# A two-layer diffusion transformer with 32 experts: rows in plain column order, weights in pairs of rows, splits 2,048 wide

## The chip, the cores and the metric

One core of a Trainium2 chip. The metric is the time of one execution on the device, in microseconds (us). TensorE (PE) multiplies; its weight loads are listed apart as PEld. VectorE (DVE), ScalarE (ACT) and GpSimd (POOL) do elementwise work, and SyncE (SP) issues most DMAs. Each engine takes its instructions strictly in the order in which the program was laid down. An instruction that has to wait holds up all those behind it on its engine.

## What is computed

Two layers over 1,024 latent tokens of width 1,024 and 256 context tokens: grouped-query attention in layer 0, a Fourier mix in layer 1, each followed by a mixture of 32 experts, of which every token uses two.

```python
for i in range(DEPTH):
    ...
    h = _modulate(x, norm_mix[i], sh1, sc1)
    ...
    x = x + g1 * y
    x = x + g2 * _hier_moe(_modulate(x, norm_ffn[i], sh2, sc2), *moe_p)
...
def expert_block(args):
    xblk, e = args
    return (jax.nn.silu(xblk @ w1[e]) * (xblk @ w3[e])) @ w2[e]
```

`w1[e]` and `w3[e]` are 1024x512 in fp32 and `w2[e]` is 512x1024, so an expert reads 6 MB.

## The kernel before

**Precision.** A product of fp32 matrices is made from high and low parts. ACT casts a weight to `wh` (a rounded type), DVE subtracts to get `wl`, and PE adds three products for each block of 128 rows: rows' high part by `wh` (L206), high by `wl` (L207), low by `wh` (L208).

**Weights of an expert.** They come in six pieces of 1 MB, two of each matrix, issued on SP's queue at L190. A piece fills a tile of 128 partitions by 2,048 values, or a list of two tiles 1,024 wide where a buffer of another phase is borrowed. A piece is split in two quarters 1,024 wide, by `quarter`: one cast (L1224) and one subtraction (L1229) each. One quarter in twelve is subtracted on POOL rather than on DVE. Five buffers of `wh` and five of `wl` (`NSP`) go round, and a quarter is prepared three ahead of its use (`AHEAD`).

**The loop over experts** (`phase_moe`). I call the halves of `w1` a0 and a1, those of `w2` b0 and b1, those of `w3` c0 and c1; a half is two quarters, 12 matmuls of 104 by 512. In steady state PE runs a0 of expert e; the four transposes `gT` of expert e-1's hidden rows (L1333); a1; the eight transposes of the next input rows (`xin`, L1304); b0 and b1 of expert e-1 into `py`; c0 and c1 of e. Each set of transposes goes to a PSUM tile `pt`, of which there are two. ACT takes the high part from it (`gh` L1336, `xh` L1305) and DVE the low part (`gl` L1337, `xl` L1306). From h1 and h3, ACT makes `s` (L1322) and DVE the hidden rows `gg` (L1325). DVE scales the output to `y`, in two operations (L1346); POOL adds it to its tokens in memory (L1347) and gathers the rows of later experts (L1293). The slot lists of coming experts come from one-hot tiles `oneh` on DVE (L1177) and products `pi` on PE (L1180).

**Column order.** A weight tile's partition p holds eight (or four) neighbouring rows of its matrix, 8 KB in a run. So the rows that meet it are kept in a permuted column order. Routing writes them so (`by_weights`, L956), with the shift B copied to that order on POOL (L929), and `gg` is permuted as it is written.

**What sets the order.** A scheduler orders the instructions of each engine when the program is built, from the order in the source, the pools' buffer counts and its own costs. Within an engine the order is then fixed.

Of the kernel before, what the change touches and what calls it, by code (L numbers as in the profile page):

```python
# [20 lines left out]
P = 128  # L21
D = 1024
# [44 lines left out]
NLATE, POOL_LAST = 5, 380  # L67
# [114 lines left out]
def load_piece(g, src, k, eng=None, order="(k p) n -> p k n"):  # L182

    t = raw_tile(g)
    eng = eng or g.nc.sync
    src = src.rearrange(order, p=P)
    ts = t if isinstance(t, list) else [t]
    k //= len(ts)
    for i, v in enumerate(ts):
        g.piece = eng.dma_start(v.rearrange("p (k n) -> p k n", k=k), src[:, k * i:k * i + k]).ins  # L190
    return t
# [728 lines left out]
def route_setup(g, mo, one, wk):  # L920
    nc, a, l = g.nc, g.a, mo.l
    r = Ctx()
    r.A2 = one.tile([P, D], F32, name="A2")
    r.B2 = one.tile([P, D], F32, name="B2")
    nf, b2 = (wk.tile([P, D], F32, name="h") for _ in range(2))
    bcast_row(g, r.A2, g.mod[l][0:1, 4 * D:5 * D])
    bcast_row(g, b2, g.mod[l][0:1, 3 * D:4 * D])
# [5 lines left out]
    for q in range(2):  # L933
        for nm, n0, n1 in (("rg", 0, NG), ("re", NG, NG + NE)):
            nc.gpsimd.dma_start(r.W[:, 4 * q:4 * q + 4, n0:n1],
                                a["moe_w_" + nm][l, q * 512:q * 512 + 512].rearrange("(p j) n -> p j n", j=4))
# [230 lines left out]
def slot_index(g, m, wk, pp, n, posm, val, tag):  # L1167

    nc = g.nc
    b = NE // 4 - 1 if n > 3 else 1  # L1170
    pi = pp.tile([CAP, n, 5], F32, name="pi")
    for e in range(n):
        oh = wk.tile([P, NT, CAP], BF, name="oneh", bufs=3)
        pe = posm(e)
        for t0, t1 in ((0, NT),) if n > 1 else ((0, NT - 2), (NT - 2, NT)):
            sh = [P, t1 - t0, CAP]
            nc.vector.tensor_tensor(oh[:, t0:t1], g.jrow[:, None, :].to_broadcast(sh),  # L1177
                                    pe[:, t0:t1, None].to_broadcast(sh), OP.is_equal)
        for t in range(NT):
            nc.tensor.matmul(pi[:, e], oh[:, t], val(e, t), start=(t == 0), stop=(t == NT - 1))  # L1180
    row = wk.tile([CAP, n], F32, name="row" + tag, bufs=1)
    nc.vector.tensor_scalar(row, pi[:, :, 1], float(SEQ), None, OP.add)
    idx = wk.tile([CAP, n], I32, name="idx" + tag, bufs=b)
    g.idx = nc.vector.tensor_add(idx, row, pi[:, :, 0]).ins
    gate = wk.tile([CAP, n], F32, name="gate" + tag, bufs=b)
    nc.vector.reduce_sum(gate, pi[:, :, 2:5], axis=AX.X)
    return idx, gate


class Moe:  # L1190
# [22 lines left out]
    def feed(self, eng=None):  # L1213

        while self.nl < min((self.ns - len(self.late)) // 2 + self.nraw, self.limit):
# [3 lines left out]
    def quarter(self, t, i):  # L1219

        nc = self.g.nc
        t = t[i] if isinstance(t, list) else t[:, i * 1024:(i + 1) * 1024]
        h, l = (self.hp.tile([P, 1024], F32R, name=n) for n in ("wh", "wl"))
        nc.scalar.copy(h, t)  # L1224
        if self.ns < NLATE:
            self.late.append((l, t, h))
            return h, l
        pool = self.ns > 11 and self.ns % 12 == 9 and (self.ns < POOL_LAST or not self.l)
        i = (nc.gpsimd if pool else nc.vector).tensor_sub(l, t, h)  # L1229
        if pool:  # L1230
            self.sub = i.ins
        else:
            self.vsub = i.ins
        return h, l

    def finish_late(self):

        for l, t, h in self.late:
            self.vsub = self.g.nc.vector.tensor_sub(l, t, h).ins
# [27 lines left out]
    def split(self, n):  # L1267

        while self.ns <= min(n, 2 * len(self.order) - 1):
            i, j = divmod(self.ns, 2)  # L1270
            self.sp[self.ns] = self.quarter(self.raw[i], j)
            if j:
                del self.raw[i]
# [3 lines left out]
    def get(self, n):  # L1277
        self.split(n + AHEAD)
        return self.sp.pop(n)

    def load(self, which, e, i, eng=None):
# [6 lines left out]
        t = load_piece(self.g, src, n // P, eng, "(p k) n -> p k n")  # L1288
# [8 lines left out]
    def xin(self, xg):  # L1297
        g, nc = self.g, self.g.nc
        xh = self.wk.tile([P, KD, CAP], F32R, name="xh")
        xl = self.wk.tile([P, KD, CAP], F32R, name="xl")  # L1300
        for q in range(2):
            pt = self.ps.tile([P, 4, CAP], F32, name="pt", bufs=2)
            for j in range(4):
                nc.tensor.transpose(pt[:, j], xg[:, (4 * q + j) * P:(4 * q + j + 1) * P], g.ident[:CAP, :CAP])  # L1304
            nc.scalar.copy(xh[:, 4 * q:4 * q + 4], pt)  # L1305
            nc.vector.tensor_sub(xl[:, 4 * q:4 * q + 4], pt, xh[:, 4 * q:4 * q + 4])  # L1306
# [12 lines left out]
    def hidden(self, h1, h3):  # L1319
# [4 lines left out]

        nc.vector.tensor_mul(gg.rearrange("t (i j p) -> t i p j", i=2, j=2), s_.rearrange("t (i p j) -> t i p j", i=2, j=2),  # L1325
                             h3.rearrange("t (i p j) -> t i p j", i=2, j=2))
        return gg

    def gT(self, gg):
        nc = self.g.nc  # L1330
        pt = self.ps.tile([P, 4, CAP], F32, name="pt", bufs=2)
        for j in range(4):
            nc.tensor.transpose(pt[:, j], gg[:, j * P:(j + 1) * P], self.g.ident[:CAP, :CAP])  # L1333
# [6 lines left out]
    def store(self, py, idx, gate):  # L1340
# [58 lines left out]
def phase_moe(g, mo, after=None, fin=None):  # L1399
# [4 lines left out]
    with mo.st as st:  # L1404
# [30 lines left out]
        for e in range(NE + 1):  # L1435
# [9 lines left out]
            if late:  # L1445
                gT = mo.gT(prev)
                py = [mo.psum("py", 2) for n in range(2)]
                for i in range(4):
                    p = mo.get(k + i)
                    for n in range(2):  # L1450
                        mo.mm(py[n], gT, p, i, n, 1)
# [39 lines left out]
            if e and not late:  # L1491
                py = [mo.psum("py", 2) for n in range(2)]
                for i in range(4):
                    p = mo.get(k + i)
                    for n in range(2):
                        mo.mm(py[n], gT, p, i, n, 1)
# [30 lines left out]
    with ExitStack() as st:  # L1527
# [10 lines left out]
        with tc.For_i(0, nx, 1):  # L1538
# [28 lines left out]
            for which in range(2):  # L1567
                hs.append(mo.psum(f"h{which}"))
                for i in range(2):
                    t = mo.load(which, bass.ds(re, 1), i)  # L1570
# [3 lines left out]
            py = [mo.psum("py", 2) for n in range(2)]  # L1574
            for i in range(2):
                t = mo.load(2, bass.ds(re, 1), i)
                for j in range(2):
                    w = mo.quarter(t, j)
                    for n in range(2):
                        mo.mm(py[n], gT, w, 2 * i + j, n, 1)  # L1580
# [531 lines left out]
```

## Time and profile before

| | |
|---|---|
| median of 3 runs | 2368.72 us (2367.48 to 2373.99) |
| the profiled execution | 2366.65 us |
| its span, first to last instruction | 2364.7 us |
| mean granted clock of PE | 0.954 |
| busy: PE, DVE, ACT, POOL | 2149.3, 1949.1, 1338.1, 1045.2 us |

The span divides into attention (to about 745 us), layer 0's projection and routing (to about 925), layer 0's experts (to about 1,500), the Fourier mix with layer 1's routing (to about 1,730) and layer 1's experts (to about 2,320). The experts are half of the time. A row of a group or timeline names the line, engine, operation and tiles of an instruction, and after an arrow in brackets what the engine waited for.

### The profile page before, as it was taken

How to read it: one execution, taken by the hardware profiler on the slowest of the kernel's cores; microseconds unless marked ns; L12 is line 12 of the kernel's file. 1: busy time of each engine (PE TensorE's matmuls, PEld its weight loads, DVE VectorE, ACT ScalarE, POOL GpSimd, SP SyncE). 2: the span in 40 equal slices, each digit the busy share in tenths (PEclk: the TensorE clock that was granted, in tenths of full speed). 3: DMA queues.
4: the chain of work that ended last, by engine and by line, in shares of the span. 5: the costliest groups of instructions: out<-in, count | busy, mean ns of one | idle time of the engine just before them, and what ended most of it. 6: DMA issues, size and time to landing. Idle time of an engine off the chain costs nothing. (4 is left out here: it accounts for less than half of the span.)

```text
span 2364.7 us, 29621 instructions
## 1 busy us (share of the span) xinstructions
PE 2149.3 (91%) x10250; PEld 1424.5 (60%) x10250; DVE 1949.1 (82%) x2822; ACT 1338.1 (57%) x1741; POOL 1045.2 (44%) x560
## 2 busy tenths in 40 slices
PE   6899999999999777999999999669699999999993
PEld 3677444444445565677777766447476777776662
DVE  4878566666675788999999999676899999998995
ACT  4733344443444235677776776443476777766773
POOL 2322566676767632334334442443233434423432
PEclk8999999999999898999999999879799999999997
DMA  8544434534333777999999999645599999999995
GB/s 304 186 160 141 165 112 134 180 112 134 115 114 129 255 250 267 359 361 331 353 345 343 362 361 336 213 192 213 218 307 348 339 343 351 354 345 347 348 366 198
DMA packets 152631, 614.22 MB, mean 260 GB/s; under 512 B 26961, under 2 KB 43993, under 8 KB 106461
## 3 DMA queue, kind: packets, MB, share of 16 engines
q1 hardware_dynamic: 110188, 546.87, 63.4%
q0 software_dynamic: 24672, 54.40, 9.0%
q10 hardware_dynamic: 17616, 11.01, 1.5%
q8 instruction: 82, 1.34, 0.2%
q14 instruction: 73, 0.59, 0.1%
HBM read 559.57 MB, written 78.44 MB: 270 GB/s over the span
## 5 line engine op out<-in xcount | busy, mean ns | idle before, releaser
L207 PE MATMUL h<-wl,xh 128*104 128x512 f32 x1024 | 411.6, 402 | 20.2 <-DVE wl L1229 16.9
L206 PE MATMUL h<-wh,xh 128*104 128x512 f32 x1024 | 410.4, 401 | 3.3 <-ACT wh L1224 3.3
L208 PE MATMUL h<-wh,xl 128*104 128x512 f32 x1024 | 406.6, 397 | 0.0
L684 POOL TENSOR_TENSOR acc<-acc,pe 128x1024 f32<-128x1024 f32 x125 | 298.8, 2391 | 96.4 <-ACT pe L673 94.0
L562 DVE TENSOR_REDUCE m<-sm 128x1 f32<-128x512 f32 x360 | 206.3, 591 | 136.4 <-PE sm L561 134.7
L673 ACT ACTIVATE pe<-st 128x1024 f32<-128x1024 f32 x160 | 163.7, 1023 | 261.8 <-PE st L659 259.9
L1293 POOL DMA_INDIRECT xg<-H,idx x64 | 116.4, 1819 | 290.8 <-PE pt L1304 182.9
L207 PEld LDWEIGHTS h<-wl,xh 128*104 128x104 f32 x1024 | 173.8, 170 | 93.5 <-DVE wl L1229 28.6
L1224 ACT CAST wh<-raw 128x1024 fp32r<-128x1024 f32 x196 | 199.8, 1054 | 48.4 <-DMA raw<-in_moe_w_dram 21.2
L1229 DVE TENSOR_TENSOR wl<-raw,wh 128x1024 fp32r<-128x1024 f32 x175 | 211.1, 1245 | 12.2 <-ACT wh L1224 12.0
L1224 ACT CAST wh<-wh 128x1024 fp32r<-128x1024 f32 x180 | 185.2, 1053 | 57.2 <-DMA wh<-in_moe_w_dram 22.8
L1229 DVE TENSOR_TENSOR wl<-wh 128x1024 fp32r<-128x1024 f32 x157 | 206.3, 1336 | 11.7 <-ACT wh L1224 11.4
L206 PEld LDWEIGHTS h<-wh,xh 128*104 128x104 f32 x1024 | 173.7, 170 | 65.9 <-ACT wh L1224 4.9
L1229 DVE TENSOR_TENSOR wl<-wl,wh 128x1024 fp32r<-128x1024 f32 x163 | 206.6, 1296 | 5.7 <-ACT wh L1224 5.4
L208 PEld LDWEIGHTS h<-wh,xl 128*104 128x104 f32 x1024 | 173.4, 169 | 59.7
L1347 POOL DMA_INDIRECT Xs<-y,idx x64 | 178.0, 2781 | 70.3 <-DVE y L1346 29.3
L1224 ACT CAST wh<-wl 128x1024 fp32r<-128x1024 f32 x172 | 177.2, 1053 | 51.8 <-PE h L208 23.9
L207 PE MATMUL py<-wl,gh 128*104 128x512 f32 x512 | 204.8, 401 | 0.2 <-DVE wl L1229 0.2
L208 PE MATMUL py<-wh,gl 128*104 128x512 f32 x512 | 202.2, 397 | 0.2 <-DVE gl L1337 0.2
L206 PE MATMUL py<-wh,gh 128*104 128x512 f32 x512 | 197.5, 404 | 2.0 <-ACT gh L1336 1.8
L664 PE MATMUL po<-pe,V 128*64 128x512 f32 x640 | 174.7, 624 | 0.4 <-ACT pe L673 0.4
L1224 ACT CAST wh<-X 128x1024 fp32r<-128x1024 f32 x124 | 129.6, 1053 | 56.3 <-PE h L208 45.3
(574 smaller groups left out, 4512.6 us busy)
## 6 DMA issues: line engine op xcount, KB each, us to landing
raw<-in_moe_w_dram SPq DMA_DIRECT2D x98, 1024.0 KB
wh<-in_moe_w_dram SPq DMA_DIRECT2D x90, 1024.0 KB
wl<-in_moe_w_dram SPq DMA_DIRECT2D x86, 1024.0 KB
qs<-in_moe_w_dram SPq DMA_DIRECT2D x96, 512.0 KB
raw<-in_w_mod_dram SPq DMA_DIRECT2D x43, 1024.0 KB
X<-in_moe_w_dram SPq DMA_DIRECT2D x37, 1024.0 KB
X<-in_moe_w_dram SPq DMA_DIRECT2D x50, 512.0 KB
QS<-qst ACTq DMA_DIRECT2D x32, 256.0 KB
```

Of the source, the lines that this page charges most:

```text
L206: nc.tensor.matmul(out, lh, wh, start=start, stop=False)
L207: nc.tensor.matmul(out, lh, wl, start=False, stop=False)
L208: nc.tensor.matmul(out, ll, wh, start=False, stop=stop)
L562: nc.vector.reduce_max(m3[:, h, qt, b:b + 1], ps[:, :kn], axis=AX.X)
L664: nc.tensor.matmul(po[64 * h:64 * h + 64], g.V[:, kt, g4 * HD:(g4 + 1) * HD], pe[:, h], start=(kt == 0), stop=(kt == NTA - 1))
L673: nc.scalar.activation(pe, ps, AF.Exp, scale=SCALE)
L684: eng.tensor_add(acc, acc, pe)
L1224: nc.scalar.copy(h, t)
L1229: i = (nc.gpsimd if pool else nc.vector).tensor_sub(l, t, h)
L1293: self.last = self.g.nc.gpsimd.indirect_dma_start(out=xg, out_offset=None, in_=self.H if src is None else src, in_offset=bass.IndirectOffs ...
L1347: return y, lambda: nc.gpsimd.indirect_dma_start(out=self.X, out_offset=bass.IndirectOffsetOnAxis(ap=idx, axis=0), in_=y, in_offset=None, ...
```

## The change

Five parts.

1. **Column order.** Routing's rows keep plain column order: `by_weights` is gone, B is loaded where it is used, and the router's weights come in 2 DMAs rather than 4.
2. **Pairs of rows.** A partition holds pairs of neighbouring rows. For `w1` and `w3` a piece is two runs of 4 KB in each partition; `w2` keeps 8 KB. The pieces in two tiles stay two DMAs with 4 KB runs.
3. **Splits in halves.** One cast and one subtraction 2,048 wide split a half (two of 1,024 each where the piece is in two tiles). Three buffers 2,048 wide take the place of five 1,024 wide, and a half is prepared two ahead. Of POOL's halves (one in six), DVE subtracts the first 1,024 and POOL the second, after one cast of 2,048.
4. **Transposes.** One `pt` tile of two banks serves `gT` and `xin` in turn. The transposes read every second value of a row. `xh` and `xl` are one operation of 832 columns each, and `gg` is a plain product.
5. **Outputs.** `py` is one tile of two banks and `y` one operation 1,024 wide.

There are also two `oneh` buffers where there were three.

```diff
-AHEAD = 3
-NSP = 5
-NSP_EARLY = 3
+NSP = 3
+NSP_EARLY = 2
...
-NLATE, POOL_LAST = 5, 380
+NLATE, POOL_LAST = 3, 190
...
-    nc.gpsimd.tensor_copy(by_weights(r.B2), b2.rearrange("t (q p j) -> t q p j", q=2, j=4))
+    bcast_row(g, r.B2, g.mod[l][0:1, 3 * D:4 * D])
...
-    x, a2 = (v[:, ns].rearrange("t (p j) -> t p j", j=4) for v in (x1, r.A2))
-    g.nc.vector.tensor_mul(by_weights(r.u[t])[:, n], x, a2)
+    g.nc.vector.tensor_mul(r.u[t][:, ns], x1[:, ns], r.A2[:, ns])
...
-        oh = wk.tile([P, NT, CAP], BF, name="oneh", bufs=3)
...
+            oh = wk.tile([P, NT, CAP], BF, name="oneh")
...
-    def quarter(self, t, i):
+    def half(self, t, ns=None):
...
-        h, l = (self.hp.tile([P, 1024], F32R, name=n) for n in ("wh", "wl"))
-        nc.scalar.copy(h, t)
...
+        h, l = (self.hp.tile([P, 2048], F32R, name=n) for n in ("wh", "wl"))
+        pool = ns is not None and ns > 5 and ns % 6 == 4 and (ns < POOL_LAST or not self.l)
...
     def get(self, n):
-        self.split(n + AHEAD)
-        return self.sp.pop(n)
+
+        i, j = divmod(n, 2)
+        self.split(i + NSP - 1)
+        return self.quarter(self.sp.pop(i) if j else self.sp[i], j)
...
-        t = load_piece(self.g, src, n // P, eng, "(p k) n -> p k n")
+        t = load_piece(self.g, src, n // P // 2, eng, "(k p j) n -> p k (j n)")
...
+        pt = self.ps.tile([P, 2, 512], F32, name="pt")
         for q in range(2):
-            pt = self.ps.tile([P, 4, CAP], F32, name="pt", bufs=2)
...
-            nc.scalar.copy(xh[:, 4 * q:4 * q + 4], pt)
-            nc.vector.tensor_sub(xl[:, 4 * q:4 * q + 4], pt, xh[:, 4 * q:4 * q + 4])
...
+        nc.scalar.copy(hv, pt)
+        nc.vector.tensor_sub(lv, pt, hv)
...
+        nc.vector.tensor_mul(gg, s_, h3)
...
-        pt = self.ps.tile([P, 4, CAP], F32, name="pt", bufs=2)
+        pt = self.ps.tile([P, 2, 512], F32, name="pt")[:, 0, :4 * CAP].rearrange("p (j n) -> p j n", j=4)
...
-        for n in range(2):
-            ns = slice(n * 512, (n + 1) * 512)
-            nc.vector.scalar_tensor_tensor(y[:, ns], py[n], gate, self.G2[:CAP, ns], OP.mult, OP.mult)
+        nc.vector.scalar_tensor_tensor(y, py.rearrange("t n c -> t (n c)"), gate, self.G2[:CAP], OP.mult, OP.mult)
```

The scheduler lays the new program down in another order. Before, DVE does this in the experts of layer 1, from one product `gg` on (`wl` is a subtraction of a weight part; the second name in each row is what it is made from):

```order
L1325 TENSOR_TENSOR gg<-s,h_18357 104x2x128x2
L1229 TENSOR_TENSOR wl<-wl,wh 128x1024
L1229 TENSOR_TENSOR wl<-raw,wh 128x1024 x2
L1337 TENSOR_TENSOR gl<-pt,gh 128x416
L1229 TENSOR_TENSOR wl<-raw,wh 128x1024 x2
L1229 TENSOR_TENSOR wl<-qs,wh 128x1024
L1306 TENSOR_TENSOR xl<-pt,xh 128x416 x2
```

In the changed kernel the same stretch of DVE is:

```order
L1339 TENSOR_TENSOR gg<-s,h_17052 104x512
L1238 TENSOR_TENSOR wl<-wl,wh 128x2048
L1238 TENSOR_TENSOR wl<-raw,wh 128x2048
L1351 TENSOR_TENSOR gl<-pt,gh 128x416
L1173 TENSOR_TENSOR oneh<-jrow,posb 128x832
L1238 TENSOR_TENSOR wl<-raw,wh 128x2048
L1321 TENSOR_TENSOR xl<-pt,xh 128x832
```

Between `gg` and `gl` stood two or three subtractions 1,024 wide; now there are in most experts two 2,048 wide.

On PE, before, at the end of a1 (the last `h`), with the input transposes (`pt` from `xg`) and the first three products of `py`:

```order
L208 MATMUL h_18412<-wh,xl 104x512
L1304 MATMUL pt<-ident,xg 128x104 x8
L206 MATMUL py<-wh,gh 104x512
L207 MATMUL py<-wl,gh 104x512
L208 MATMUL py<-wh,gl 104x512
```

And PE at the same place in the changed kernel:

```order
L210 MATMUL h_17595<-wh,xl 104x512
L208 MATMUL py<-wh,gh 104x512
L209 MATMUL py<-wl,gh 104x512
L1317 MATMUL pt<-ident,xg 128x104 x8
L210 MATMUL py<-wh,gl 104x512
```

The input transposes moved behind the first two products of `py`; in about twenty experts two groups of `pi` stand there too, between those products and the transposes. On ACT the cast of b1 stands ahead of `gh`, as it did before for its first quarter.

## Rows read from the trace of the kernel before

**Rows 1.** windows view of line 1325: stretch, us, busy (count), clock, DMA, GB/s

```profile
924.40:1493.90 569.50, 32.57 (x30) 0.99 0.98 350
1731.50:2299.30 567.80, 32.57 (x30) 1.00 0.99 348
```

**Rows 2.** same stretches, busy of PE, PEld, DVE, ACT, POOL

```profile
924.40:1493.90 569.50, 553.84 (x2710) 401.73 (x2709) 551.09 (x572) 415.70 (x479) 220.61 (x87) 0.99 0.98 350
1731.50:2299.30 567.80, 550.29 (x2704) 399.00 (x2702) 543.83 (x578) 415.82 (x479) 211.27 (x87) 1.00 0.99 348
```

**Rows 3.** waits of PE, layer 0: line, releaser: us, times, longest

```profile
PE h L207 <- DVE wl L1229: 10.1, 15, 1.7
...
PE pt L1304 <- DVE gl L1337: 1.2, 1, 1.2
```

**Rows 4.** timeline of PE, one expert: start us, us, instruction [idle before]

```profile
2053.83 0.58 PE L1333 MATMUL pt<-ident,gg 104*128 104x104 f32 x4 [0.91 <-DVE gg L1325]
...
2054.48 0.39 PE L207 MATMUL h<-wl,xh 128*104 128x512 f32 x1
...
2056.79 0.40 PE L208 MATMUL h<-wh,xl 128*104 128x512 f32 x1
...
2057.02 0.88 PE L1304 MATMUL pt<-ident,xg 104*128 104x104 f32 x8
...
2057.68 0.46 PE L206 MATMUL py<-wh,gh 128*104 128x512 f32 x1
```

**Rows 5.** timeline of ACT, same expert

```profile
2057.22 0.60 ACT L1322 ACTIVATE s<-h 104x512 f32<-104x512 f32 x1 [0.34 <-PE h L208]
```

**Rows 6.** timeline of DVE, same expert

```profile
2052.73 1.04 DVE L1325 TENSOR_TENSOR gg<-s,h 104x512 f32<-104x512 f32 x1
...
2053.62 2.33 DVE L1229 TENSOR_TENSOR wl<-wl,wh 128x1024 fp32r<-128x1024 f32 x2
...
2055.88 0.57 DVE L1337 TENSOR_TENSOR gl<-pt,gh 128x416 fp32r<-128x416 f32 x1
...
2066.26 1.40 DVE L1346 SCALAR_TENSOR_TENSOR y<-py,gate,G 104x512 f32<-104x512 f32 x2
```

**Rows 7.** groups by form: ns min/median/max, first and last start us

```profile
L1229 DVE TENSOR_TENSOR wl<-wl,wh x161: 1198/1216/3420, 929.3 to 2296.9; 128x1024 fp32r<-128x1024 f32 x161
...
L201 DVE TENSOR_TENSOR wl<-raw,wh x8: 2228/2292/3857, 31.5 to 747.7; 128x2048 fp32r<-128x2048 f32 x8
...
L200 ACT CAST wh<-raw x8: 1894/1908/1917, 29.6 to 744.8; 128x2048 fp32r<-128x2048 f32 x8
...
L1177 DVE TENSOR_TENSOR oneh<-jrow,posb x66: 360/1015/1971, 891.4 to 2113.5; 128x832 bf16<-128x832 bf16 x62, 128x624 bf16<-128x624 bf16 x2, 128x208 bf16<-128x208 bf16 x2
```

**Rows 8.** groups by form, plain operations 512 and 1,024 wide

```profile
L880 DVE TENSOR_TENSOR X<-mm,G x16: 653/681/692, 754.2 to 875.5; 128x512 f32<-128x512 f32 x16
...
L1983 DVE SCALAR_TENSOR_TENSOR X<-X,ftrs,V x8: 1277/1280/1287, 2330.9 to 2345.8; 128x1024 f32<-128x1024 f32 x8
```

**Rows 9.** group by form, weight loads of the input transposes

```profile
L1304 PEld LDWEIGHTS pt<-ident,xg x512: 137/140/231, 899.3 to 2287.8; 104*128 104x128 f32 x171
```

**Rows 10.** timelines of POOL and of DVE, both splitting

```profile
1239.24 2.62 POOL L1229 TENSOR_TENSOR wl<-raw,wh 128x1024 fp32r<-128x1024 f32 x1 [6.86 <-ACT wh L1224]
...
1239.51 3.44 DVE L1229 TENSOR_TENSOR wl<-raw,wh 128x1024 fp32r<-128x1024 f32 x1
```

**Rows 11.** groups by form, routing: rows into weight order, and the copy of B

```profile
L956 DVE TENSOR_TENSOR h<-X,A x32: 1032/1098/2884, 757.2 to 1685.8; 128x512 f32<-128x512 f32 x32
...
L929 POOL COPY B<-h x2: 2032/3007/3982, 745.6 to 1613.8; 128x1024 f32<-128x1024 f32 x2
```

**Rows 12.** windows view, all engines, layer 0's projection and routing

```profile
745.00:868.00 123.00, 101.61 (x483) 79.30 (x482) 105.44 (x168) 36.70 (x61) 84.20 (x58) 0.92 0.66 227
```

**Rows 13.** page, DMA queues: packets, MB, share of engines

```profile
q1 hardware_dynamic: 110188, 546.87, 63.4%
...
q10 hardware_dynamic: 17616, 11.01, 1.5%
```

More of the change, by code (lines that the diff above doesn't have):

```diff
@@ L924, in route_setup @@
     r.B2 = one.tile([P, D], F32, name="B2")
-    nf, b2 = (wk.tile([P, D], F32, name="h") for _ in range(2))
+    nf = wk.tile([P, D], F32, name="h")
     bcast_row(g, r.A2, g.mod[l][0:1, 4 * D:5 * D])
-    bcast_row(g, b2, g.mod[l][0:1, 3 * D:4 * D])
     bcast_row(g, nf, a["norm_ffn"][l:l + 1])
-    nc.gpsimd.tensor_copy(by_weights(r.B2), b2.rearrange("t (q p j) -> t q p j", q=2, j=4))
+    bcast_row(g, r.B2, g.mod[l][0:1, 3 * D:4 * D])
     r.gain = lambda: nc.vector.scalar_tensor_tensor(r.A2, r.A2, 1.0, nf, OP.add, OP.mult)
@@ L932, in route_setup @@
     nc.gpsimd.memset(r.W, 0.0)
[L933 to L936, printed above, removed]
+    nc.gpsimd.dma_start(r.W[:, :, 0:NG], a["moe_w_rg"][l].rearrange("(k p) n -> p k n", p=P))
+    nc.gpsimd.dma_start(r.W[:, :, NG:NG + NE], a["moe_w_re"][l].rearrange("(k p) n -> p k n", p=P))
     r.bias = one.tile([P, NG + NE], F32, name="br")
@@ L1172, in slot_index @@
     for e in range(n):
-        oh = wk.tile([P, NT, CAP], BF, name="oneh", bufs=3)
+        if e == 2 and n == 3:
+            oh = wk.tile([P, DE], F32, name="gg", bufs=1).bitcast(BF)[:, :NT * CAP].rearrange("p (t c) -> p t c", t=NT)
+        else:
+            oh = wk.tile([P, NT, CAP], BF, name="oneh")
         pe = posm(e)
@@ L1213, in feed, with rest, quarter @@
     def feed(self, eng=None):
-        while self.nl < min((self.ns - len(self.late)) // 2 + self.nraw, self.limit):
+        while self.nl < min(self.ns - len(self.late) + self.nraw, self.limit):
             self.raw[self.nl] = self.load(*self.order[self.nl], eng)
             self.nl += 1
-    def quarter(self, t, i):
+    def half(self, t, ns=None):
         nc = self.g.nc
-        t = t[i] if isinstance(t, list) else t[:, i * 1024:(i + 1) * 1024]
-        h, l = (self.hp.tile([P, 1024], F32R, name=n) for n in ("wh", "wl"))
-        nc.scalar.copy(h, t)
[L1225 to L1231, printed above, removed]
-        else:
-            self.vsub = i.ins
-        return h, l
+        h, l = (self.hp.tile([P, 2048], F32R, name=n) for n in ("wh", "wl"))
+        pool = ns is not None and ns > 5 and ns % 6 == 4 and (ns < POOL_LAST or not self.l)
+        if isinstance(t, list):
+            todo = [(l[:, c:c + 1024], v, h[:, c:c + 1024], pool and c) for c, v in zip((0, 1024), t)]
+        elif pool:
+            nc.scalar.copy(h, t)
+            todo = [(v[0], v[1], v[2], c) for c in (0, 1024) for v in [[u[:, c:c + 1024] for u in (l, t, h)]]]
+        else:
+            todo = [(l, t, h, 0)]
+        if isinstance(t, list) or not pool:
+            for v in todo:
+                nc.scalar.copy(v[2], v[1])
+        if ns is not None and ns < NLATE:
+            self.late.append(todo)
+        else:
+            self.rest(todo)
+        return h, l
+    def rest(self, todo):
+        for l, t, h, pool in todo:
+            i = (self.g.nc.gpsimd if pool else self.g.nc.vector).tensor_sub(l, t, h).ins
+            if pool:
+                self.sub = i
+            else:
+                self.vsub = i
+    @staticmethod
+    def quarter(t, j):
+        return [v[:, 1024 * j:1024 * j + 1024] for v in t]
     def finish_late(self):
-        for l, t, h in self.late:
-            self.vsub = self.g.nc.vector.tensor_sub(l, t, h).ins
+        for todo in self.late:
+            self.rest(todo)
         self.late = []
@@ L1267, in split @@
     def split(self, n):
[L1269 to L1273, printed above, removed]
+        while self.ns <= min(n, len(self.order) - 1):
+            self.sp[self.ns] = self.half(self.raw.pop(self.ns), self.ns)
             self.ns += 1
@@ L1446, in phase_moe @@
                 gT = mo.gT(prev)
-                py = [mo.psum("py", 2) for n in range(2)]
+                py = mo.ps.tile([CAP, 2, 512], F32, name="py")
                 for i in range(4):
@@ L1491, in phase_moe @@
             if e and not late:
-                py = [mo.psum("py", 2) for n in range(2)]
+                py = mo.ps.tile([CAP, 2, 512], F32, name="py")
                 for i in range(4):
@@ L1569, in phase_moe @@
                 for i in range(2):
-                    t = mo.load(which, bass.ds(re, 1), i)
+                    t = mo.half(mo.load(which, bass.ds(re, 1), i))
                     for j in range(2):
@@ L1573, in phase_moe @@
             gT = mo.gT(mo.hidden(*hs))
-            py = [mo.psum("py", 2) for n in range(2)]
+            py = mo.ps.tile([CAP, 2, 512], F32, name="py")
             for i in range(2):
-                t = mo.load(2, bass.ds(re, 1), i)
+                t = mo.half(mo.load(2, bass.ds(re, 1), i))
                 for j in range(2):
```

27 lines of the change are left out of this document (15 added, 12 removed).

## The prediction

> **What bounds the kernel now.** I read the windows view first, because the change lies almost wholly in the two loops over experts, and counted experts by their `gg`. Thirty go by in 569.50 us in layer 0 and in 567.80 us in layer 1 [rows 1], so an expert takes 18.98 and 18.93 us, and there are about 62 such periods in steady state. In the same stretches PE is busy for 553.84 and 550.29 us [rows 2]: 18.46 and 18.34 us an expert, with 0.52 and 0.58 us idle. DVE is busy for 551.09 and 543.83 us, and the DMA engines for 0.98 and 0.99 of the time. So three resources are full, and PE is the one with nothing left to give: its products alone, 72 at the step of 0.231 us (ten steps from 2054.48 to 2056.79 [rows 4]), are 16.63 us. What little PE waits for is mostly `wl` from DVE (10.1 us in fifteen waits). For the product `gl` ahead of the input transposes it waited once, 1.2 us [rows 3].
>
> Next I read the timelines of one expert, to see how `gl` is hidden. PE begins the transposes of the hidden rows at 2053.83 and gets to the input transposes at 2057.02 [rows 4]. DVE makes two quarter subtractions in 2.33 us after `gg`, then `gl`, which ends at 2055.88 + 0.57 = 2056.45 [rows 6]. So `gl` is 0.57 us early. This is the slack that the change has to live in.
>
> **The waits inside the new order.** This is the term that decides. Between `gg` and `gl` DVE now subtracts b0 and b1 whole. Three buffers go round, a0, a1, b0, so the cast of b1 takes the buffer of a0, and that is free when PE ends a0, just as it begins the hidden transposes (call this 0). A product's result releases ACT 0.20 us after the next instruction of PE has begun: next at 2057.02 [rows 4], `s` at 2057.22 [rows 5]. A 2,048-wide cast takes 1.91 us and a 2,048-wide subtraction 2.29 us (medians, rows of the attention phase), against 1.216 us for a quarter [rows 7]. So b1 is cast by 0.20 + 1.91 = 2.11 and subtracted by 4.40, and `gl` ends at 4.40 + 0.57 - 0.08 (two operations of DVE overlap at their joint: 2053.62 + 2.33 against 2055.88 [rows 6]) = 4.9. PE needs it after the hidden transposes and a1, 2057.02 - 2053.83 = 3.19 [rows 4], and two products of `py`, 0.46: at 3.65. There is now one `pt` tile, so the input transposes wait for `gl`; and the third product of `py` reads `gl` itself, so a second tile would gain little. The stall is 4.9 - 3.65 = **1.3 us an expert**, on PE, the engine with no slack. Queued behind it on PE are `py` and c0 and c1. DVE has gone on, but its next `xl` waits too.
>
> In before the buffers went round in quarters: the cast of b1's first quarter waited for half of a0, not all of it, and `gl` came ahead of b1's second quarter.
>
> How much of the 1.3 us shows? If nothing else of PE's idle time remains, the period is 18.46 + 1.3 = 19.76 and 18.34 + 1.3 = 19.64, which is 0.78 and 0.71 above before. If the old idle time stays on top, it is 1.3. If the stall hides wholly behind something, 0. I take 0.75, because the old waits are mostly for `wl` [rows 3], and a PE that arrives later finds those done. 62 x 0.75 = **+46 us** (0 to +81).
>
> **The one-hot tiles.** In about twenty experts two groups of `pi` stand between the two products and the input transposes, and the second reads a `oneh` that DVE makes behind `gl`, 1.015 us [rows 7]. The first `pi` group fills part of the stall. I count 0.5 us in each, **+10 us** (0 to +20).
>
> **What gets shorter on DVE.** A half is one subtraction of 2.29 us rather than two in 2.33; `y` is one of 1.28 (the 1,024-wide row [rows 8]) rather than 1.40 [rows 6]; `gg` falls from 1.04 [rows 6] to the plain 0.68 [rows 8]. With six halves that is 0.2 + 0.1 + 0.4 = 0.7 us an expert, `xl` a little besides. It lies beside PE's work except for `gg`, which the hidden transposes wait for. That wait was 0.91 us in the expert shown [rows 4], but all that PE idles is 0.5 us an expert [rows 2], and mostly for `wl` [rows 3], so I cost the gain at nothing in the sum. It is the first rival's ground.
>
> **Routing.** 32 operations wrote rows in weight order, at 1.098 us; plain ones of that size take 0.681 [rows 11, 8]. That is 32 x 0.42 = 13 us of DVE, and the two copies of B (2.0 and 4.0 us on POOL) go. In layer 0's stretch DVE is busy for 105.44 of 123 us [rows 12]; I let half count: **-7 us** (0 to -18).
>
> **Loads.** At most 256 pieces (four in each of 64 experts; those in two tiles have 4 KB already) change from 128 packets of 8 KB to 256 of 4 KB. From the two queues' rows [rows 13], a packet of 4,963 bytes took 218 ns of one engine (63.4% of 16 x 2,364.7 us by 110,188) and one of 625 bytes 32 ns. A line through both leaves some 5.5 ns that a packet costs whatever its size; 256 x 128 x 5.5 / 16 ns = 11 us. PE's stall gives DMA time to catch up, so I take **+3 us** (0 to +11).
>
> **Strided transposes.** The twelve transposes of an expert now read every second value. No row shows PE do that. The nearest is the write in weight order on DVE, 1.6 times the plain one. At that ratio the eight input transposes (0.66 us [rows 4]) and the four others would cost about 0.6 us an expert, +37 us; at the other end nothing, since what is read strided is the loaded operand (0.137 us [rows 9]), and loads run under the product before. I take 0 and keep the other end for the range.
>
> The Trainium skill (SBUF — State Buffer, Specifications (TRN2)) says that SBUF lines are 16 bytes and that full bandwidth wants at least two accesses in each. Steps of 16 bytes have one, and the old write in weight order was slow as that says. Steps of 8 bytes have two, so by this rule the transposes cost nothing, the end that I took.
>
> **The sum.** Against the profiled execution, 2366.65 us: +46 + 10 - 7 + 3 = +52 gives 2418.7. That execution is 2.1 us under the median of its runs, so a median of 2,420.8, say **2420 us**, +2.2%.
>
> **Rival 1: DVE's relief wins.** If the early experts are paced by DVE (0.97 busy [rows 2]), its 0.7 us come back as period, and if scheduling slack hides `gl`, PE sinks toward its busy time: 0.52 x 62 = -32, and -7 from routing, about 2330 us. For it: DVE is as full as PE. Against it: an in-order engine is held by its place in the chain, and b1's cast cannot start before a0 is done. It decides if `gl` ends less than 3.65 us after the hidden transposes begin, as when DVE does `gl` ahead of b1, which a few of the rows of the new order do. Chance 0.2.
>
> **Rival 2: the stall is covered.** DMA is at 0.98 of its time; if its arrivals set the period, PE's new stall takes the place of waits for weights, and only routing and the loads show: 2366.65 - 7 + 3 + 2.1, about 2365 us. For it: the full DMA engines. Against it: PE's idle time was half a microsecond, and the stall is more than twice that. Chance 0.1.
>
> **Rival 3: POOL and DVE block one another.** Where both subtracted at once, POOL took 2.62 us and DVE 3.44 against 1.216 [rows 10, 7]: DVE lost 2.2 us. Before, `y` stood beside most of POOL's work. Now DVE's 1,024 and POOL's are released by one cast, and a 2,048-wide subtraction follows `y` and stands ahead of `gg`. If one more microsecond is lost there in half of the experts, that is +31: about 2450 us. Chance 0.15.
>
> The Trainium skill (SBUF — State Buffer, SBUF: two separate sides) has a rule for this: DVE with two SBUF inputs and GpSimd take a shared port pair as an exclusive lock, for the whole instruction, and the other blocks. The 3.44 us agree: 2.2 us of waiting and 1.2 of work. By that rule, a wider DVE operation makes POOL wait longer too.
>
> **How the numbers follow.** Forecast as summed 0.55, rivals 0.2, 0.1 and 0.15. The range runs from **2345**, which takes in the part of rival 1 where some of the stall shows, to **2455**, which holds rival 3 and half of the price of strided transposes. A measurement of this kernel tells 0.3% (7 us) from no change: faster 0.2, same 0.1, slower 0.7.
>
> **What would show it.** Right: in the new trace the input transposes (or `pi`) wait for `gl` (or `oneh`) about 1 to 1.5 us in most experts, `gl` ends 4.5 to 5 us after the hidden transposes begin, the period is 19.5 to 20, and DMA's share falls under 0.96. Wrong: `gl` ends before PE's second product of `py`, or the period stays under 19 with DVE below 0.95. The strided transposes are shown by eight in more than 0.66 us; the loads, by waits for DMA.

## The result: slower, by less than half of the forecast

The changed kernel takes 2392.45 us (median of four runs, 2388.91 to 2395.71) against 2368.44 us for the kernel before (2367.48 to 2373.99). The ratio is 1.0096, with a 95% interval of 1.0072 to 1.012: 17 to 28 us slower. The forecast was slower, by 52 us, and the range of 2345 to 2455 holds the time. The size is off by a factor of two, and the parts of the sum are further off than the sum.

The profiled execution took 2388.91 us, its span 2386.7 us. The windows view again, line of `gg` (1339 now), thirty experts of each layer; it answers to [rows 1]:

```profile
912.30:1499.60 587.30, 20.22 (x30) 0.99 0.98 340
1732.80:2316.50 583.70, 20.24 (x30) 1.00 0.99 342
```

An expert takes 587.30 / 30 = 19.58 us and 19.46 us, 0.59 and 0.53 more than before: 34 us in all. The first `gg` comes at 912.3 rather than 924.4, and about 5 us are lost after the last.

All engines in the same stretches (busy of PE, PEld, DVE, ACT, POOL), which answers to [rows 2]:

```profile
912.30:1499.60 587.30, 566.67 (x2713) 414.35 (x2712) 523.67 (x381) 397.22 (x288) 257.02 (x88) 0.99 0.98 340
1732.80:2316.50 583.70, 562.29 (x2700) 410.85 (x2698) 523.66 (x407) 399.28 (x315) 243.67 (x88) 1.00 0.99 342
```

DVE's work fell as it should, from 551 us to 524 us in layer 0. DVE had time left and the kernel was slower. What PE and its weight loads wait for in layer 0 (line, releaser: us, times, longest) answers to [rows 3]:

```profile
PE pt L1317 <- DVE gl L1351: 15.4, 22, 1.7
PE pt L1347 <- DVE gg L1339: 2.4, 2, 1.2
PE h L209 <- DVE wl L1238: 1.3, 1, 1.3
...
PEld pt L1317 <- DVE gl L1351: 21.7, 23, 2.2
PEld pt L1347 <- DVE gg L1339: 14.0, 27, 1.6
```

The wait for `gl` ahead of the input transposes is now first, and the waits of products for `wl` went from 10.1 us to 1.3. The timelines of one expert of layer 1, on DVE, ACT and PE, answer to [rows 4 to 6]:

```profile
2080.83 0.68 DVE L1339 TENSOR_TENSOR gg<-s,h 104x512 f32<-104x512 f32 x1
2081.43 2.29 DVE L1238 TENSOR_TENSOR wl<-wl,wh 128x2048 fp32r<-128x2048 f32 x1
2084.21 2.29 DVE L1238 TENSOR_TENSOR wl<-wh 128x2048 fp32r<-128x2048 f32 x1 [0.50 <-ACT wh L1229]
2086.42 0.58 DVE L1351 TENSOR_TENSOR gl<-pt,gh 128x416 fp32r<-128x416 f32 x1
...
2082.28 1.91 ACT L1229 CAST wh<-wh 128x2048 fp32r<-128x2048 f32 x1 [0.90 <-PE h L210]
2084.09 0.50 ACT L1350 CAST gh<-pt 128x416 fp32r<-128x416 f32 x1
...
2082.03 0.61 PE L1347 MATMUL pt<-ident,gg 104*128 104x104 f32 x4
...
2085.50 0.40 PE L209 MATMUL py<-wl,gh 128*104 128x512 f32 x1
2087.06 1.20 PE L1317 MATMUL pt<-ident,xg 104*128 104x104 f32 x8 [1.16 <-DVE gl L1351]
```

This is the chain of the prediction, step for step. The hidden transposes begin at 2082.03. The cast of b1, released by the end of a0, begins 0.25 us later (forecast 0.20); b1 is subtracted from 2084.21 to 2086.50; `gl` ends at 2087.00, 4.97 us after the transposes began (forecast 4.9); PE stands still for 1.16 us after the end of its product. Counted from start to start, as the forecast was, the step from 2085.50 to 2087.06 is 1.33 us longer than a product's 0.231 (forecast 1.3). What the timeline of one expert can't say is how many experts look like this.

So I took the start times of PE's instructions and summed, for each kind, what a step took beyond its usual 0.231 us. A step is charged to the instruction that came late. Us an expert, layer 0 / layer 1:

| | before | changed |
|---|---|---|
| period | 18.98 / 18.93 | 19.58 / 19.46 |
| the twelve transposes, running | 1.05 / 1.07 | 1.45 / 1.44 |
| late: input transposes | 0.03 / 0.03 | 0.64 / 0.61 |
| late: hidden transposes | 0.05 / 0.13 | 0.21 / 0.17 |
| late: products of h1 and h3 | 0.71 / 0.63 | 0.18 / 0.27 |
| late: products of `py` | 0.19 / 0.14 | 0.18 / 0.14 |

Three things happened. PE waits 0.6 us for `gl`; its transposes take 0.4 us longer; and 0.4 to 0.5 us of its old waits are gone. One sign that the prediction named did not come: DMA's share was to fall under 0.96, and it stayed at 0.98 and 0.99, while the rate fell from 350 and 348 GB/s to 340 and 342.

### The profile page after: what moved, and what is told of

The parts are those of the page before. It is cut to its first block, busy times and chain, and to the rows that moved or that the text cites. A ratio compares the mean times of both kernels' runs of the same rounds, so it can differ in the third digit from the quotient of the medians.

```text
span 2386.7 us, 28590 instructions
## 1 busy us (share of the span) xinstructions
PE 2172.0 (91%) x10250; PEld 1451.9 (61%) x10250; DVE 1884.7 (79%) x2432; ACT 1296.6 (54%) x1363; POOL 1098.8 (46%) x554
## 5 line engine op out<-in xcount | busy, mean ns | idle before, releaser
L1304 POOL DMA_INDIRECT xg<-H,idx x64 | 127.4, 1990 | 365.9 <-PE pt L1317 281.6
L1238 DVE TENSOR_TENSOR wl<-raw,wh 128x2048 fp32r<-128x2048 f32 (+1 forms) x97 | 215.0, 2221 | 51.9 <-ACT wh L1229 41.4
L1238 DVE TENSOR_TENSOR wl<-wh 128x2048 fp32r<-128x2048 f32 (+1 forms) x90 | 209.6, 2329 | 39.4 <-ACT wh L1229 32.4
L1359 POOL DMA_INDIRECT Xs<-y,idx x64 | 202.0, 3157 | 48.9 <-DVE y L1358 32.8
L208 PE MATMUL py<-wh,gh 128*104 128x512 f32 x512 | 206.7, 404 | 11.3 <-ACT gh L1350 8.3
L1238 DVE TENSOR_TENSOR wl<-wl,wh 128x2048 fp32r<-128x2048 f32 (+1 forms) x85 | 185.8, 2185 | 23.2 <-ACT wh L1229 16.4
L1229 ACT CAST wh<-raw 128x2048 fp32r<-128x2048 f32 x82 | 156.1, 1905 | 85.9 <-PE h L210 48.1
L1229 ACT CAST wh<-wh 128x2048 fp32r<-128x2048 f32 x81 | 154.5, 1907 | 76.3 <-PE h L210 47.5
L1229 ACT CAST wh<-wl 128x2048 fp32r<-128x2048 f32 x69 | 131.5, 1906 | 70.5 <-PE h L210 46.1
L1238 DVE TENSOR_TENSOR wl<-X,wh 128x1024 fp32r<-128x1024 f32 (+1 forms) x90 | 143.4, 1612 | 21.2 <-ACT wh L1229 13.0
```

The lines of the kernel that those rows point to most:

```text
L208: nc.tensor.matmul(out, lh, wh, start=start, stop=False)
L1229: nc.scalar.copy(v[2], v[1])
L1238: i = (self.g.nc.gpsimd if pool else self.g.nc.vector).tensor_sub(l, t, h).ins
L1304: self.last = self.g.nc.gpsimd.indirect_dma_start(out=xg, out_offset=None, in_=self.H if src is None else src, in_offset=bass.IndirectOffs ...
L1359: return y, lambda: nc.gpsimd.indirect_dma_start(out=self.X, out_offset=bass.IndirectOffsetOnAxis(ap=idx, axis=0), in_=y, in_offset=None, ...
```

## The experiments

Every time is the median beside that of the kernel before on the same chip; the ratio goes by those. The changed kernel's own ratio is 1.0096.

### Taking the wait for gl away: e1, e3, e13

e1 lays `gh` and `gl` down ahead of b1's split:

```diff
-        self.split(i + NSP - 1)
+        with ExitStack() as st:
+            for x in self.gx:
+                st.enter_context(self.g.tc.issue_after(x))
+            self.split(i + NSP - 1)
...
-        nc.scalar.copy(gh, pt)
-        nc.vector.tensor_sub(gl, pt, gh)
+        self.gx = (nc.scalar.copy(gh, pt).ins, nc.vector.tensor_sub(gl, pt, gh).ins)
```

> The changed kernel, with the high and low parts of the hidden rows (gh on ACT, gl on DVE) laid down ahead of the cast and subtraction of b1. Theory (the order costs): in the changed kernel's trace PE's step from the second product of py to the input transposes is 1.07 us too long in 13 of layer 0's 30 experts and 0.42 us in 12 more, 0.62 us an expert in both layers, some 37 us of the program. With gl first that wait should fall under 0.1 us an expert and the time by 25 to 37 us, to 2355 to 2368. Rival (the width costs): a 2,048-wide split makes some other product late in its place, PE's waits for wl or wh grow by as much, and the time stays at 2385 to 2392.

2375.36 us against 2366.93, ratio 1.0040 (1.0026 to 1.0055). Against the changed kernel's ratio 0.56% less, 13 us. Waits of PE and PEld in e1, layer 0:

```profile
PE h L209 <- DVE wl L1239: 5.1, 11, 0.8
PE pt L1351 <- DVE gg L1343: 4.4, 5, 1.2
PE py L209 <- DVE wl L1239: 2.2, 3, 0.9
...
PEld h L209 <- DVE wl L1239: 14.7, 31, 1.2
```

The wait for `gl` is gone (input transposes late by 0.02 and 0.07 us an expert). But products now wait for `wl` again: 0.42 and 0.58 us an expert, where the changed kernel had 0.18 and 0.27. Both expectations got half.

e3 leaves the order and gives the hidden transposes a PSUM tile of their own:

```diff
-        pt = self.ps.tile([P, 2, 512], F32, name="pt")[:, 0, :4 * CAP].rearrange("p (j n) -> p j n", j=4)
+        pt = self.ps.tile([P, 4, CAP], F32, name="gp")
```

> The changed kernel, with a PSUM tile of its own for the hidden rows' transposes, so that the input transposes need not wait for gl. What the prediction said: it gains little (under 5 us), since the third product of py reads gl. Rival: the input transposes, about 0.95 us, fit into the gap of 1.07 us, so the wait nearly goes: 20 to 35 us less, 2357 to 2372.

2378.21 us against 2366.93, ratio 1.0055 (1.0037 to 1.0073): about 10 us less than the changed kernel. The prediction's sentence that a second tile would gain little is wrong: about 0.95 us of transposes fit into the gap ahead of `py`'s third product, and the scheduler put them there. Products of h1 and h3 wait for weights again here too, 0.46 and 0.52 us an expert.

e13 does both, for the question that was left: are these two waits all that wide splits cost?

> The changed kernel, with gh and gl ahead of b1's split (as e1) and a PSUM tile of their own for the hidden rows' transposes (as e3). Theory (these two waits are what wide splits cost): it comes near e4_quarters, 2363 to 2370. Rival (wide splits make other products late too, as the waits for weights in e1 and e3 hint, 0.4 to 0.6 us an expert against 0.18 to 0.27 in the changed kernel): it stays at 2373 to 2380, no better than e1.

2377.86 us against 2365.6, ratio 1.0055 (1.0035 to 1.0076): no better than either, as the rival said. Waits in e13, layer 0, and then the same waits in e4, which has the narrow splits of before (next section):

```profile
PE h L209 <- DVE wl L1239: 8.8, 14, 1.5
PE h L209 <- POOL wl L1239: 1.8, 3, 0.6
...
PE h L210 <- DVE wl L1226: 5.2, 10, 0.8
PE h L210 <- POOL wl L1226: 3.2, 5, 0.7
```

The rival's time came, but not its mechanism. Products of h1 and h3 are late by 0.57 us an expert in both layers of e13, and by 0.56 and 0.59 in e4, where splits are narrow. The windows of thirty experts in each layer, e13 and then e4, lie close together:

```profile
916.10:1492.10 576.00, 20.34 (x30) 1.00 1.00 344
1730.40:2308.10 577.70, 20.35 (x30) 1.00 0.99 342
...
915.00:1488.60 573.60, 20.32 (x30) 1.00 0.99 346
1719.50:2294.50 575.00, 20.41 (x30) 0.99 0.99 344
```

The same sums for the other kernels, and what is left of each span (us, one execution of each):

| | before | changed | e1 | e3 | e13 | e4 |
|---|---|---|---|---|---|---|
| sixty experts | 1137.3 | 1171.0 | 1150.8 | 1153.9 | 1153.7 | 1148.6 |
| the rest of the span | 1227.4 | 1215.7 | 1224.3 | 1225.4 | 1220.3 | 1212.5 |

In the sixty experts the changed kernel loses 22 us to e4, and without the wait for `gl` 17 (e3, e13) to 20 (e1) of these come back. The times show only 10 to 13 because e1, e3 and e13 lose 5 to 10 us outside the experts. Most of that lies at the start of the Fourier mix: in all three the last store of layer 0 (`Xs`) waits for the store before it to land, and the first products of the mix (`u`) come later. e13, and then the changed kernel:

```profile
POOL Xs L1362 <- DMA Xs<-y,idx: 6.6, 1, 6.6
PE u L1726 <- ACT bsh L1690: 16.4, 1, 16.4
...
PE u L1723 <- ACT bsh L1687: 10.7, 1, 10.7
```

The changed kernel and e4 have no such wait of the store, and 10.7 us at `u`; the kernel before has 7.3 and 16.3. No run varies that store alone.

### Quarters again, and halves alone: e4, e5

e4 is the changed kernel with the splits of before, 1,024 wide in five buffers:

```diff
-NSP = 3
-NSP_EARLY = 2
+AHEAD = 3
+NSP = 5
+NSP_EARLY = 3
...
-        h, l = (self.hp.tile([P, 2048], F32R, name=n) for n in ("wh", "wl"))
...
+        h, l = (self.hp.tile([P, 1024], F32R, name=n) for n in ("wh", "wl"))
```

> The changed kernel, with splits of 1,024 in five buffers as in the kernel before, all the rest as changed. Theory (the order that wide splits bring costs): gl comes ahead of b1's second quarter again, PE's wait for it goes, and the gains elsewhere stay (routing 16 us): 2352 to 2372, at or under the kernel before; strided transposes still cost. Rival (the rest costs, 4 KB runs and strided reads above all): 2380 to 2395.

2363.24 us against 2366.93, ratio 0.9987 (0.9974 to 1.0001). So all of the change but the width of the splits is worth about -3 us, and the wide splits (with their three buffers) about +26. In the profiles the -3 is 11 us more in the sixty experts and 15 us less outside them. The input transposes are late by 0.09 and 0.12 us an expert, and the shared `pt` tile is still there: what made it hurt was `gl` behind two subtractions of 2.29 us.

e5 is the other side, the kernel before with nothing but the wide splits (and two `oneh` buffers):

```diff
-AHEAD = 3
-NSP = 5
-NSP_EARLY = 3
+NSP = 3
+NSP_EARLY = 2
...
-        h, l = (self.hp.tile([P, 1024], F32R, name=n) for n in ("wh", "wl"))
...
+        h, l = (self.hp.tile([P, 2048], F32R, name=n) for n in ("wh", "wl"))
```

> The kernel before, with splits 2,048 wide in three buffers and two one-hot buffers, as in the change; rows, loads, transposes and outputs as before. Theory: gl falls behind b1's subtraction as in the changed kernel; PE waits some 0.6 us an expert for it and 0.5 us of its old waits for wl go, so 0.1 to 0.3 us an expert are left: 6 to 20 us slower, 2373 to 2387. Rival (wide splits are all of the loss): 2388 or more. Rival (DVE's shorter work wins): 2360 or less.

2383.52 us against 2366.61, ratio 1.0071 (1.0054 to 1.0088): 17 us, as expected in size, but not by the mechanism that I gave. Waits in layer 0:

```profile
PE pt L1350 <- DVE gg L1342: 11.8, 18, 1.7
PE h L206 <- DVE wl L1244: 9.5, 14, 2.2
...
PEld pt L1350 <- DVE gg L1342: 20.0, 18, 2.2
PEld h L206 <- DVE wl L1244: 19.6, 36, 2.6
```

With two `pt` tiles PE doesn't wait for `gl` (0.04 and 0.06 us an expert). It waits for `gg`, 0.50 and 0.42 us, because a wide subtraction stands ahead of it on DVE and `gg` is still the slow permuted product (1,060 ns). One expert, DVE and then PE:

```profile
1001.08 2.28 DVE L1244 TENSOR_TENSOR wl<-wl,wh 128x2048 fp32r<-128x2048 f32 x1
1003.28 1.05 DVE L1342 TENSOR_TENSOR gg<-s,h 104x512 f32<-104x512 f32 x1
...
1004.38 0.58 PE L1350 MATMUL pt<-ident,gg 104*128 104x104 f32 x4 [1.45 <-DVE gg L1342]
```

So a wide split costs wherever the short product behind it is the one that PE needs; which product that is depends on the rest.

### The other parts: e2, e8, e6

e2 is the changed kernel with its transposes reading neighbours:

```diff
-                nc.tensor.transpose(pt[:, q, j * CAP:j * CAP + CAP], v[:, j // 2, j % 2], g.ident[:CAP, :CAP])
+                nc.tensor.transpose(pt[:, q, j * CAP:j * CAP + CAP], xg[:, q * 512 + j * P:q * 512 + j * P + P], g.ident[:CAP, :CAP])
...
-            nc.tensor.transpose(pt[:, j], v[:, j // 2, j % 2], self.g.ident[:CAP, :CAP])
+            nc.tensor.transpose(pt[:, j], gg[:, j * P:j * P + P], self.g.ident[:CAP, :CAP])
```

> The changed kernel, with all twelve transposes of an expert reading neighbouring values rather than every second one. The rows then meet the wrong weights, so the values are not the reference's; every instruction is there in its size. Theory (strided reads cost PE): in the changed kernel a transpose step is 0.13 to 0.14 us against 0.09 to 0.11 before, some 0.4 us an expert, 25 us in all. The hidden rows' part lies ahead of the wait for gl and is swallowed by it where there is one; so 14 to 25 us come back: 2367 to 2378. Rival (the longer steps are only waits for weights loads or for pt): no change, 2388 to 2396.

2381.15 us against 2366.93, ratio 1.0064 (1.0047 to 1.0081): 0.32% less than the changed kernel, 8 us. The transposes fell from 1.45 and 1.44 us an expert to 1.05 and 1.04, which would be 24 us in sixty experts; but the waits for `gl` and `gg` grew by 0.1 to 0.2 us each. Weight loads of the input transposes, the changed kernel and e2 (ns min/median/max), for [rows 9]:

```profile
L1317 PEld LDWEIGHTS pt<-ident,xg x512: 194/218/230, 887.9 to 2303.5; 104*128 104x128 f32 x171
...
L1317 PEld LDWEIGHTS pt<-ident,xg x512: 137/140/231, 895.7 to 2302.0; 104*128 104x128 f32 x171
```

A load of a strided operand takes 218 ns rather than 140, and a step in a row of transposes 120 ns rather than 89 (medians). That the load sets the step is my reading: nothing else in these instructions changed.

e8 is the kernel before with the routing part alone:

```diff
...
-    x, a2 = (v[:, ns].rearrange("t (p j) -> t p j", j=4) for v in (x1, r.A2))
-    g.nc.vector.tensor_mul(by_weights(r.u[t])[:, n], x, a2)
+    g.nc.vector.tensor_mul(r.u[t][:, ns], x1[:, ns], r.A2[:, ns])
...
```

> The kernel before, with only the routing part of the change: rows in plain column order, B loaded where it is used, the router's weights in two loads. The experts then meet rows in another order than their weights, so values are not the reference's; the work is the same. Theory: the first product of the experts came 12 us earlier in the changed kernel, and layer 1's routing took 4 us less, all of it from this: 10 to 18 us faster, 2349 to 2357. Rival (the early start comes from fewer splits ahead of the first expert): under 5 us.

2361.36 us against 2366.61, ratio 0.9972 (0.9961 to 0.9983): 4 to 9 us faster, less than I read from the two profiles. The first `gg` of a profile is a poor measure: it stands at 924.4 in the kernel before, at 918.0 in e8, but also at 919.9 in e5 and 916.1 in e6, which route as before.

e6 is the kernel before with the loads of the change:

```diff
...
-        t = load_piece(self.g, src, n // P, eng, "(p k) n -> p k n")
+        t = load_piece(self.g, src, n // P // 2, eng, "(k p j) n -> p k (j n)")
```

> The kernel before, with only the pairs of rows: loads of w1 and w3 in two runs of 4 KB for each partition rather than one of 8 KB. The rows then meet the wrong weights, so values are not the reference's. Theory (each packet has a fixed price, and DMA sets the pace of the last twenty experts of each layer): the two kernels with 2 KB runs had 79,000 more packets than theirs with 4 KB and lost about 25 us; 26,000 more packets are then worth some 8 us: 2370 to 2380. Rival (down to 4 KB a packet's price is hidden): within 3 us of the kernel before.

2372.21 us against 2368.16, ratio 1.0021 (1.0002 to 1.0040): between nothing and 9 us. Where it lies is plain in the windows of the first ten and the last twenty experts of layer 0 (line of `gg`: us, busy (count), clock, DMA share, GB/s), before and then e6:

```profile
924.40:1113.20 188.80, 10.91 (x10) 0.99 0.98 348
1113.20:1493.90 380.70, 21.66 (x20) 1.00 0.99 350
...
916.10:1104.80 188.70, 10.89 (x10) 0.99 0.99 347
1104.80:1492.30 387.50, 21.66 (x20) 1.00 1.00 344
```

The first ten don't feel it: in the kernel before, ACT's casts wait 1 us in all for loads there, and 18 us in the last twenty. The last twenty of e6 lose 6.8 us.

### Shorter runs: e7, c2

e7 is the changed kernel with single rows in a partition, so that transposes read neighbours and every row still meets its own weights; c2 is the same with quarters.

```diff
...
-        t = load_piece(self.g, src, n // P // 2, eng, "(k p j) n -> p k (j n)")
+        t = load_piece(self.g, src, n // P, eng, "(k p) n -> p k n")
...
```

> The changed kernel, with single rows in a partition: loads of w1 and w3 in runs of 2 KB and of w2 in 4 KB, and all transposes reading neighbouring values; values are the reference's. Theory: reading neighbours gives back the 9 us that it gave alone, and packets cost their fixed 5.5 ns each only where DMA sets the pace: 2375 to 2385. Rival (DMA sets the pace): up to 28 us more, 2390 to 2410.

> The changed kernel, with splits of 1,024 in five buffers as before, and single rows in a partition (2 KB runs, plain transposes); values are the reference's. Theory: the 26 us that quarters gave and the part of the strided reads that shows in it (0.25 us an expert, 15 us): 2345 to 2358, under both kernels. Rival (more packets cost as DMA sets the pace, now that PE waits less): 2365 to 2385.

2406.39 us, ratio 1.0173 (1.0156 to 1.0190), and 2389.51 us, ratio 1.0099 (1.0082 to 1.0116), both against 2366.61. Each is some 26 us over its fellow with 4 KB runs and plain transposes (e2) or 4 KB runs (e4). My theory that packets would hardly count fell; the rival holds. c2, layer 0, first ten and last twenty:

```profile
916.90:1106.60 189.70, 6.78 (x10) 0.99 1.01 341
1106.60:1499.20 392.60, 13.55 (x20) 1.00 1.01 339
```

### Does the load set the pace? e10, e11

Both load only a sixteenth of each piece of `w2` and read it sixteen times; e10 is the kernel before, e11 the changed one.

```diff
...
+        if which == 2 and not isinstance(e, bass.DynSlice):
+            t = raw_tile(self.g)
+            t = t[0] if isinstance(t, list) else t
+            self.g.piece = self.piece = (eng or self.g.nc.sync).dma_start(t[:, :128], src[0:P, :128]).ins
+            return (t,)
```

> The kernel before, with only a sixteenth of each piece of w2 loaded and read sixteen times (values are not the reference's): a third less to load, all else in its size. Theory (DMA sets the pace of the last twenty experts, and so covers part of a stall on PE): their period falls from 19.04 and 18.96 to 18.4 to 18.8, and the time to 2345 to 2358. Rival (it is DVE and PE that set it): the period stays within 0.1, 2362 or more.

> The changed kernel, with the same lighter loads of w2. Theory (its period is set by PE with its wait for gl and its longer transposes, not by loads): it stays within 0.15 of 19.39 and 19.48, at 2380 to 2392, and the distance to the lighter kernel before grows from 24 to 30 us or more, as the cover is gone. Rival (the loads set the pace of both): both fall by as much.

e10: 2346.05 us against 2368.16, ratio 0.9912 (0.9885 to 0.9939). e11: 2395.68 us, ratio 1.0126 (1.0078 to 1.0173), no faster than the changed kernel with all its loads. Layer 0, first ten and last twenty, e10 and then e11:

```profile
919.30:1108.00 188.70, 10.88 (x10) 0.99 0.78 255
1108.00:1480.00 372.00, 21.63 (x20) 1.00 0.79 254
...
917.20:1115.60 198.40, 6.75 (x10) 0.99 0.74 242
1115.60:1505.70 390.10, 13.49 (x20) 1.00 0.77 242
```

With a third less to load the kernel before gains 8.7 us in the last twenty experts and nothing in the first ten: there, loads set 0.4 us of its period. The changed kernel gains nothing anywhere. It has left the loads behind and is held by its own chain. The distance grows from 24 to 50 us. So loads covered up to half of what the change really costs PE; in the sixty experts alone the distance grows from 34 to 52 us, and a third was covered.

### A version that beats both: e9, and e12

e9 is e4 with the 8 KB loads of the kernel before; the input transposes then read every fourth value.

```diff
-        t = load_piece(self.g, src, n // P // 2, eng, "(k p j) n -> p k (j n)")
+        t = load_piece(self.g, src, n // P, eng, "(p k) n -> p k n")
...
-            v = xg[:, q * 512:q * 512 + 512].rearrange("t (k p j) -> t k j p", k=2, j=2)
+            v = xg[:, q * 512:q * 512 + 512].rearrange("t (p j) -> t j p", j=4)
...
```

> As e4_quarters, but with the loads of the kernel before (8 KB runs), so that the input transposes read every fourth value, 16 bytes apart, and the hidden rows' every second; values are the reference's. Theory (packets): the 26,000 packets fewer give 4 to 9 us over e4_quarters, 2354 to 2360, if a step of 16 bytes costs PE no more than one of 8. Rival (the wider step is dearer, as it is in DVE's writes): eight transposes at 1.6 times the 8-byte price are 0.5 us an expert more, 2375 or more.

2361.75 us against 2368.16, ratio 0.9981 (0.9966 to 0.9996): 1 to 8 us faster than the kernel before, and some 27 us faster than the changed one. The last twenty experts go at 381.0 us where e4 has 383.1 and 384.4. The wider step is no dearer (and the write on DVE that the expectation compares it with steps by 128 values, 512 bytes):

```profile
L1303 PEld LDWEIGHTS pt<-ident,xg x512: 194/217/231, 892.0 to 2282.7; 104*128 104x128 f32 x171
...
L1303 PEld LDWEIGHTS pt<-ident,xg x512: 195/218/231, 896.0 to 2278.9; 104*128 104x128 f32 x171
```

These are e4 (steps of 8 bytes) and e9 (16 bytes). e12 asks what the strided reads cost where no stall swallows them: e4 with the edit of e2.

> As e4_quarters (splits of 1,024, the rest as changed), with all transposes reading neighbouring values; values are not the reference's. Theory: e4's transposes took 1.30 us an expert against 1.05; with no stall to swallow it, the first ten experts of each layer gain all 0.25 us and the last twenty, where loads set the pace, little: 3 to 8 us under e4's 2363, at 2355 to 2360. Rival (the whole 0.25 us counts in every expert): 15 us, 2348. Rival (strided reads are hidden altogether): within 2 us of e4.

2363.13 us against 2365.6, ratio 0.9989 (0.9972 to 1.0007), against e4's 0.9987: nothing, the last of the three expectations. In the trace the first ten experts go at 188.8 and 187.7 us rather than 190.5 and 190.6, so 0.17 to 0.29 us an expert are there. The last twenty, which wait for loads anyway, give nothing (385.0 and 383.7 against 383.1 and 384.4).

## Why the forecast had the sign and not the size

**The wait for `gl`: mechanism right, size wrong (+46 us, the step "the stall is 1.3 us an expert").** The chain is as I worked it out, to a tenth of a microsecond where it occurs. But I took one expert's order for all sixty. In 26 of the sixty nothing stands between `py`'s first products and the transposes, and the step there is 1.04 us too long in the mean (1.09 to 1.88 us in 21 of them, 0.33 or less in five). In 20 more the groups of `pi` stand in the gap and only some 0.43 us are left. In 14 the transposes stand ahead of `py`, and there is next to none. The mean is 0.62 us, not 1.3. The rows of the new order showed these kinds; I had used them for the first rival and not for the sum.

**What the stall displaces.** I took 0.52 us an expert of old waits to vanish, and 0.36 to 0.53 did. Net of that the stall costs 0.1 to 0.25 us an expert, 6 to 15 us, where I had 46. By e1 and e13, sixty experts without it are 20 and 17 us shorter, some 5 us of that in the transposes themselves; the time fell by 13 and 10. Either way it is under half of 46. e10 and e11 show why old waits could vanish: in the last twenty experts the kernel before was waiting for loads.

**The strided transposes: priced at nothing, and 0.4 us an expert (the step "I take 0").** My upper bound was 0.6 us, by the ratio of DVE's strided write. My reason for the lower end was that loads run under the product before; in a row of eight transposes there is no long product to run under. The Trainium skill (SBUF — State Buffer, Specifications (TRN2)), by which two accesses in a 16-byte line give full bandwidth, disagrees with the trace here: 8-byte steps took 218 ns against 140, and 16-byte steps the same. The old write in weight order, which the prediction set beside that rule, is no example of 16-byte steps: `by_weights` steps by 128 values, 512 bytes. In the changed kernel the strided reads are worth 8 us (e2). They made up, by chance, for a part of the first error.

**One-hot tiles: +10 us forecast, none found.** The `pi` groups filled the gap rather than lengthening it.

**Routing: -7 us forecast.** e8 has -4 to -9. **Loads: +3 us forecast, 0 to +11.** e6 has 0 to +9.

**Rivals.** DVE's relief bought nothing: DVE fell from 0.97 to 0.89 busy and the period grew. The second rival, a stall covered by loads, held in part, as e10 and e11 show. The third is in the trace and off the path: POOL's subtractions take 3,442 ns in the median of a group where the shortest takes 2,619, but PE's waits list none of them in either layer's experts.

**The sum, from the runs.** Wide splits alone +17 us (e5), loads +5 (e6), routing -5 (e8): +17. The strided reads add 8 in the changed kernel (e2) and nothing in e4 (e12). All parts but the splits together are worth -3 (e4), so in their company the splits cost 26. Most of that is the one wait for `gl`: in the sixty experts 17 to 20 of the 22 us between the changed kernel and e4. It needs both the order that wide splits bring (e1) and the shared `pt` tile (e3), for either edit takes it away. e13 stays 16 us over e4 in time; 5 us of that are in the sixty experts and some 6 at the late start of the Fourier mix; the rest is spread over the span, and no run separates it. Wide splits with four buffers weren't tried, so what is due to the width and what to having three buffers stays open.

## What to carry to other kernels

Making two operations into one saved 0.04 us at a subtraction and 0.12 at `y`, and doubles the time that a short, urgent operation behind it may have to wait; look at what stands behind the long one before counting the saving. Count how many rounds of a loop have the order that you worked out, not whether one has. And ask of each stretch what else holds it: where loads set the pace, both a gain and a loss on an engine are covered, so a part's price differs between the first ten and the last twenty experts of one loop. When an experiment gives back less than its trace says, look outside the loop before naming another cost inside it: e1 and e3 lost, at the start of the Fourier mix, some 5 of the 17 to 20 us that they won in the experts.

## What the runs showed of the hardware

A transpose's weight load (104x128) takes 140 ns for neighbouring fp32 values (e2) and 217 to 218 ns for every second (e4) or every fourth (e9), 8 or 16 bytes apart.

With the DMA engines full, the last twenty experts of layer 0 moved 350 GB/s in runs of 8 KB (the kernel before and e9), 344 to 347 with `w1` and `w3` in 4 KB (e6, e4), and 334 to 339 with 2 KB for those and 4 KB for `w2` (e7, c2).
